# Rectified row sums: clamping on ScalarE and summing on VectorE, four rows per instruction, with three input buffers

## The chip, the cores and the metric

The kernel runs on one core of one Trainium2 chip. The metric is the device time of one execution in microseconds.

## The reference

```python
def setup_inputs():
    batch, seq, dim = 32, 512, 1024
    return {"x": np.random.randn(batch, seq, dim).astype(np.float32)}

def reference(x):
    relu_x = np.maximum(x, 0)
    return np.sum(relu_x, axis=-1).astype(np.float32)
```

There are 16,384 rows of 1024 fp32 numbers, 67.1 MB. Each of the 128 partitions takes 128 rows that follow one another in memory.

## The kernel before

Seven blocks of 16 rows per partition (4 KB a row, so 64 KB per partition) go through two buffers. Then come pieces of 8, 4, 2 and 1 rows, and the last row in four parts. Even rows go to ScalarE, odd rows to VectorE; each row is one instruction that clamps and sums. The sums gather in `res`, one column per row.

```python
io_pool = ctx.enter_context(tc.tile_pool(name="io", bufs=2))
# ... act_op: scalar.activation(Relu, accum_out=res[:, m])
# ... dve_op: vector.tensor_scalar(max 0, add, accum_out=...)
for j, cpd in enumerate(chunks):                 # 16 x 7, then 8, 4, 2, 1
    # ... xt = a buffer of the pool
    nc.sync.dma_start(out=xt, in_=...)
    for c in range(cpd):
        m = m0 + c
        if m == NT - 2:                          # row 126, ScalarE's last
            act_op(xt[:, c, :], xt[:, c, :], m)
            nc.scalar.dma_start(out=out2d[:, 0 : NT - 2], in_=res[:, 0 : NT - 2])
        elif (c % 2) == 0:
            act_op(xt[:, c, :], xt[:, c, :], m)
        else:
            dve_op(xt[:, c, :], xt[:, c, :], res[:, m : m + 1])
    m0 += cpd
# ... row 127 in four parts on VectorE
nc.sync.dma_start(out=out2d[:, NT - 2 : NT], in_=res[:, NT - 2 : NT])
```

The scheduler puts ScalarE's output DMA ahead of ScalarE's last row. In ScalarE's stream stand, one after the other, a separate semaphore wait (an instruction of its own that does nothing but wait for another engine's signal; the trace has it at 158.38 us, 0.02 us long) for VectorE's last full row (row 13 of the tail, row 125 in all), the issue of the output DMA, and row 126.

## Time and profile before

| | before |
|---|---|
| device time | 164.37 us (164.32 to 164.52) |
| span | 162.7 us |
| load queue busy | 96.4% of 16 DMA engines' span |
| VectorE, ScalarE busy | 46%, 42% |
| last load packet ends | 159.3 us |
| last output DMA issued | 160.44 us |

From the page of the kernel before: span and busy times, the DMA queues (packets, MB, share), the chain that ended last by engine, and the two main groups of instructions (count, busy us, mean ns of one, idle before and what ended it).

```profile
span 162.7 us, 347 instructions
DVE 74.3 (46%) x134; ACT 69.0 (42%) x129; POOL 0.2 (0%) x4
...
q1 hardware_dynamic: 2304, 67.11, 96.4%
q10 hardware_dynamic: 144, 0.06, 0.1%
q14 instruction: 2, 0.02, 0.0%
...
DMA 78%; DVE 18%; SPq 1%; issue 0%; DVEq 0%
...
L49 DVE TENSOR_SCALAR_CACHE_REDUCE xt<-xt 128x1024 f32<-128x1024 f32 x63 | 72.6, 1215 | 85.7 <-DMA xt<-in_x_dram 85.4
L41 ACT ACTIVATE xt<-xt 128x1024 f32<-128x1024 f32 x64 | 66.7, 1043 | 90.3 <-DMA xt<-in_x_dram 90.3
```

The loads (q1) fill the span, and both engines wait for them more than they work.

The end of the timeline of the kernel before (start us, duration us, engine, line, operation; ACTq and SPq are DMA issues):

```profile
158.44 0.37 ACTq L73 DMA_DIRECT2D out_dram<-res  x1
...
158.85 1.06 ACT L41 ACTIVATE xt<-xt 128x1024 f32<-128x1024 f32 x1 [0.58 <-DMA xt<-in_x_dram]
...
159.82 0.19 ACT L41 ACTIVATION_READ_ACCUMULATOR xt<-xt 128x1 f32 x1
...
160.29 0.08 DVE L49 DVE_READ_ACCUMULATOR p<-p 128x1 f32 x1
160.44 0.35 SPq L98 DMA_DIRECT2D out_dram<-res  x1
```

ScalarE ends its last row at 160.0, VectorE its last part at 160.37, and the last output goes out at once.

### The profile page before, as it was taken

The numbers are of one execution on the slowest core, as the hardware profiler recorded it, in microseconds if no ns is written. First come the engines' busy times: TensorE is split into PE (matmuls) and PEld (weight loads), VectorE is DVE, ScalarE is ACT, GpSimd is POOL, SyncE is SP. The second block draws the span as 40 slices with busy tenths as digits, with TensorE's granted clock in tenths as the row PEclk, the third lists the DMA queues.
The fourth block names the chain that finished last, engine by engine and source line by source line (L and its number), as shares of the span: only waits on it lengthen the run. The fifth ranks groups of instructions, "written<-read, shape, count | busy, mean of one in ns | idle before, by whom it ended". The sixth has DMA issues, their size and how long they took to land.

```text
span 162.7 us, 347 instructions
## 1 busy us (share of the span) xinstructions
DVE 74.3 (46%) x134; ACT 69.0 (42%) x129; POOL 0.2 (0%) x4
## 2 busy tenths in 40 slices
DVE  0000029900597007950099300992039900598983
ACT  3000029700595007930099100990039700596882
POOL 0000000000000000000000000000000000000000
DMA  7969969969969979979989998998997997999990
GB/s 258 483 290 516 499 274 516 499 274 516 500 274 516 516 306 467 516 338 435 516 356 421 499 403 387 516 419 354 516 467 306 516 467 306 451 443 395 405 362 23
DMA packets 2450, 67.19 MB, mean 413 GB/s; under 512 B 528, under 2 KB 1040, under 8 KB 1168
## 3 DMA queue, kind: packets, MB, share of 16 engines
q1 hardware_dynamic: 2304, 67.11, 96.4%
q10 hardware_dynamic: 144, 0.06, 0.1%
q14 instruction: 2, 0.02, 0.0%
HBM read 67.11 MB, written 0.07 MB: 413 GB/s over the span
## 4 chain that ended last, share of the span: by engine, by line
DMA 78%; DVE 18%; SPq 1%; issue 0%; DVEq 0%
DMA xt<-in_x_dram 62%; DVE xt L49 17%; DMA p<-in_x_dram 17%; SPq L65 1%; DVE p L49 1%; DVEq L49 0%; DVEq L124 0%
## 5 line engine op out<-in xcount | busy, mean ns | idle before, releaser
L49 DVE TENSOR_SCALAR_CACHE_REDUCE xt<-xt 128x1024 f32<-128x1024 f32 x63 | 72.6, 1215 | 85.7 <-DMA xt<-in_x_dram 85.4
L41 ACT ACTIVATE xt<-xt 128x1024 f32<-128x1024 f32 x64 | 66.7, 1043 | 90.3 <-DMA xt<-in_x_dram 90.3
L41 ACT ACTIVATION_READ_ACCUMULATOR xt<-xt 128x1 f32 x64 | 11.9, 186 | 0.0
L49 DVE DVE_READ_ACCUMULATOR xt<-xt 128x1 f32 x63 | 5.2, 83 | 0.0
L49 DVE TENSOR_SCALAR_CACHE_REDUCE p<-p 128x244 f32<-128x244 f32 (+3 forms) x4 | 1.6, 420 | 0.5 <-DMA p<-in_x_dram 0.4
L41 ACT ACT_TABLE_LOAD x1 | 1.3, 1283 | 0.7 <-PEq L113 0.7
L49 DVE DVE_READ_ACCUMULATOR p<-p 128x1 f32 x4 | 0.3, 83 | 0.0
L113 POOL MEMSET const-bfloat16-1.0<- 128x1 bf16 x1 | 0.1, 102 | 0.0
L113 POOL MEMSET const-uint8-127<- 128x1 uint8 x1 | 0.1, 101 | 0.0
L113 POOL MEMSET const-float32-0.0<- 128x1 f32 x1 | 0.1, 99 | 0.2 <-issue 0.2
L113 POOL MEMSET const-float32-1.0<- 128x1 f32 x1 | 0.1, 98 | 0.0
## 6 DMA issues: line engine op xcount, KB each, us to landing
xt<-in_x_dram SPq DMA_DIRECT2D x1, 4096.0 KB, 19.7
xt<-in_x_dram SPq DMA_DIRECT2D x1, 2048.0 KB, 24.2
xt<-in_x_dram SPq DMA_DIRECT2D x1, 1024.0 KB, 26.2
xt<-in_x_dram SPq DMA_DIRECT2D x1, 512.0 KB, 27.0
p<-in_x_dram SPq DMA_DIRECT2D x1, 134.0 KB, 10.0
p<-in_x_dram SPq DMA_DIRECT2D x1, 130.0 KB, 26.5
p<-in_x_dram SPq DMA_DIRECT2D x1, 126.0 KB, 26.7
p<-in_x_dram SPq DMA_DIRECT2D x1, 122.0 KB, 26.9
```

The lines of the kernel that those rows point to most:

```text
L41: nc.scalar.activation(out=out_ap, in_=in_ap, func=mybir.ActivationFunctionType.Relu, accum_out=res[:, m : m + 1],)
L49: nc.vector.tensor_scalar(out=out_ap, in0=in_ap, scalar1=0.0, scalar2=None, op0=mybir.AluOpType.max, op1=mybir.AluOpType.add, accum_out=ac ...
L65: nc.sync.dma_start(out=xt, in_=xv[:, m0 * D : (m0 + cpd) * D].rearrange("p (c d) -> p c d", c=cpd),)
L113: nc = _bacc.Bacc("TRN2", target_bir_lowering=False, num_devices=1)
```

## The change

The intent is fewer and longer instructions, with the buffer room to let the two engines work one behind the other. In six of the eight blocks ScalarE clamps four rows in one instruction (128x4096), and VectorE sums these four rows in one `tensor_reduce`. Since a buffer is then held longer, there are three of 64 KB in place of two. Block 6 and the tail keep the row instructions; the tail's pieces share one of the three buffers. The core of the diff (helpers renamed and the last row's parts are cut):

```diff
-    io_pool = ctx.enter_context(tc.tile_pool(name="io", bufs=2))
+    io = ctx.enter_context(tc.tile_pool(name="io", bufs=3))
...
+    for j in range(nbig):
+        m0 = j * ROWS
+        xt = io.tile([P, ROWS, D], fp32, tag="io", name=f"xt{j}")
+        nc.sync.dma_start(out=xt, in_=xv[:, m0 : m0 + ROWS, :])
+        if j < nbig - 1:
+            for c in range(0, ROWS, STEP):
+                rows = xt[:, c : c + STEP, :]
+                nc.scalar.activation(
+                    out=rows, in_=rows, func=mybir.ActivationFunctionType.Relu
+                )
+                nc.vector.tensor_reduce(
+                    out=res[:, m0 + c : m0 + c + STEP],
+                    in_=rows,
+                    axis=mybir.AxisListType.X,
+                    op=mybir.AluOpType.add,
+                )
         else:
+            # block 6: rows by turns, as before
...
+        if c0 + n == ROWS - 1:
+            nc.scalar.dma_start(out=out2d[:, : NT - 2], in_=res[:, : NT - 2])
```

## The prediction

> **What bounds the kernel now.** The input stream. The DMA queue table shows the load queue busy for 96.4% of the 162.7 us span (67.11 MB, 413 GB/s); only the start and the last 3.5 us lack DMA. The chain of waits is 78% DMA. Its 17% on VectorE only says that a buffer release issued a load; that load still had about 10 us of an earlier one in front of it (a 4 MB load takes 29.5 us from issue to landing, but one lands every 19.5 us: 23.2, 42.7, ... 120.75, 140.1). Both engines are half idle: per 16-row block each works about 9.2 us (timeline: VectorE rows 1.14 us apart, ScalarE rows 1.04 us apart), then waits 10 us for DMA.
>
> **What the change does in blocks 0 to 5.** It removes 48 row instructions and their accumulator reads on each engine, and adds 24 ScalarE clamps (128x4096) and 24 VectorE sums (128x4096), one behind the other; each engine now touches every row.
> - A clamp: the trace has 1.040 us for 1024 elements.[...]
> - A sum: the trace's pitch for 1024 elements is 1.14 us[...].[...] Estimate: 4.35 us each, 17.4 us a block, starting 3.6 us after the landing: buffer free 21 us after landing, against 9.2 now.
>
> VectorE's 17.4 us still fits the 19.5 us block period. A release 21 us after landing would starve two buffers, but there are three: load j+3 is issued about 21 us after block j landed, when block j+2 still has some 18 us to run. So the stream stays unbroken: same bytes, same pieces, no gain in DMA time, the only thing to gain.
>
> **The tail.** Block 5 lands at 120.75; VectorE ends its sums near 141.9 (124.4 + 4 x 4.35), 1.7 us after block 6 landed. From there VectorE is continuously busy: block 6 rows to 151, the 8-row piece to 155.6, 4-row to 157.9, row 13 to 159.0 (before: 158.35). The large output DMA on ScalarE's queue waits for row 13, and ScalarE's last row stands behind it: it ends near 160.6 (before 160.0); the four pieces on VectorE near 160.5 (before 160.37). The last output is issued 0.2 to 0.4 us later. Every 0.1 us more per sum adds 0.4 us here.
>
> **Prediction:** 164.8 us, range 164.2 to 166.0. Faster by over 2%: 1%; within 2%: 94%; slower by over 2%: 5%.
>
> **What would show it.** Right: load queue still busy about 96%, a 4 MB landing every 19.5 us; loads landing about 40 us after issue; clamps near 3.6 us, sums near 4.35 us; VectorE busy about 127 us, ScalarE about 107 us; VectorE's first row of block 6 about 1.7 us late.
> Wrong: sums over 4.87 us (19.5 / 4): VectorE then falls behind at each block, takes over the chain, and the time rises over 2%. Or clamps waiting for sums of the same tile (8 us per four rows, 32 us a block); the built order shows no such wait. Or DMA packets that slow down while both engines sweep each tile. Or faster landings from three queued loads, which I do not expect: the DMA engines already have no pauses.

The forecast's clamp, the "3.6 us after the landing", was 3.60 us, 3.51 us apart, 14.1 us a block, not shown then. The 4.35 us of a sum is close to what the row instructions of VectorE in the trace of the kernel before give as an estimate, 4.32 us for 4096 elements (the next one starts 1.14 us after a row of 1024 elements and 0.33 us after a part of 244, so 1.04 ns an element and 0.08 us for each). That `tensor_reduce` keeps this pace was an assumption, not shown then. With 3.6 us and four times 4.35 us, VectorE ends block 5's sums near 141.9 us, the last output comes 0.2 to 0.4 us later, and the forecast came to 164.8 us, 0.4 above the 164.4 of the kernel before.

## More of the kernel before

The issue of the large output DMA takes 0.37 us of ScalarE's queue.

## The result and the profile after

The changed kernel is correct and takes 166.16 us (166.14 to 166.17), against 164.34 us for the kernel before in the same rounds. Ratios here are the mean time of one kernel's fast runs over that of the other's of the same rounds, so not quite the ratio of the medians that are quoted: 1.0113, 95% interval 1.0099 to 1.0127. That is inside 2%, but above the predicted range of 164.2 to 166.0, and the rise of 1.8 us is about four times the predicted 0.4.

The page after:

```profile
span 164.4 us, 203 instructions
DVE 123.0 (75%) x62; ACT 103.3 (63%) x57; POOL 0.2 (0%) x4
...
q1 hardware_dynamic: 2304, 67.11, 95.3%
q10 hardware_dynamic: 144, 0.06, 0.1%
q14 instruction: 2, 0.02, 0.0%
...
L70 DVE TENSOR_REDUCE res<-xt 128x4 f32<-128x4096 f32 x24 | 104.4, 4412 | 36.6 <-ACT xt L67 36.6
L67 ACT ACTIVATE xt<-xt 128x4096 f32<-128x4096 f32 x24 | 84.8, 3604 | 47.3 <-DMA xt<-in_x_dram 47.3
```

Up to the tail all is as predicted: a clamp takes 3.60 us and a sum 4.41 us, VectorE still waits before each of the blocks 0 to 5 (36.6 us in six waits), and the loads are about as dense as before (load queue busy 95.3% of the span in place of 96.4%; a block lands every 19.4 us in place of 19.5). By the DMA records the last load packet even ends at 158.9 us, 0.4 us earlier than in the profile of before. The time is lost behind that point. The end of the chain of waits after (start us, us, what; ACTq is ScalarE's queue, "issue" is time without a wait that the profile shows):

```profile
150.13 7.99 DVE tail L48 x14
158.13 0.02 issue
158.15 0.02 ACTq L96
158.16 0.35 issue
158.51 2.37 ACTq L96
160.88 0.05 issue
160.93 1.06 ACT tail L40
161.98 0.09 ACTq L138
```

And the end of the timeline after:

```profile
158.51 2.37 ACTq L96 DMA_DIRECT2D out_dram<-res  x1
...
159.90 0.08 DVE L48 DVE_READ_ACCUMULATOR p<-p 128x1 f32 x1
160.93 1.06 ACT L40 ACTIVATE tail<-tail 128x1024 f32<-128x1024 f32 x1 [3.05 <-DVE p L48]
161.89 0.19 ACT L40 ACTIVATION_READ_ACCUMULATOR tail<-tail 128x1 f32 x1
162.10 0.35 SPq L112 DMA_DIRECT2D out_dram<-res  x1
```

VectorE is done at 159.98, earlier than before (160.37). ScalarE's issue of the output DMA, the same 63 KB as before, takes 2.37 us in place of 0.37, and a gap of 0.35 us precedes it. ScalarE's last row stands behind that issue, and the last output behind the row: it is issued at 162.10 in place of 160.44. The note "3.05 <-DVE p L48" on the last row misleads: ScalarE did not need VectorE's parts, it was in its own queue's DMA issue.

What went on during the issue? The DMA queues of the changed kernel between 158.5 and 160.9 us:

```profile
q14 instruction: 1, 0.01, 1.4%
q1 hardware_dynamic: 14, 0.01, 1.3%
```

One packet of q14 falls into the issue; its record gives 8,192 bytes, from 159.17 to 159.72 us. In the kernel before, both q14 packets came near 85 and 88 us. The trace calls their kind "instruction". So I took them for refills of the engines' instruction streams. "Refill" below is my name for such a packet: no trace shows what it carries, but the experiments test the reading by moving the packets.

Counted in the trace from 0, the held issue is instruction 63 of ScalarE (an accumulating activation counts as two, as in the trace). Before, it was number 136. So the theory was: the change made ScalarE's stream shorter, and by that moved a refill from the middle of the kernel onto the issue at its end. The rival: something else in the changed kernel (third buffer, deeper load queue, sums written in strips) makes the issue long.

### The profile page after: what moved, and what is told of

It is laid out like the page before. It is cut to its first block, busy times and chain, and to the rows that moved or that the text cites. A ratio compares the mean times of both kernels' runs of the same rounds, so it can differ in the third digit from the quotient of the medians.

```text
span 164.4 us, 203 instructions
## 1 busy us (share of the span) xinstructions
DVE 123.0 (75%) x62; ACT 103.3 (63%) x57; POOL 0.2 (0%) x4
## 3 DMA queue, kind: packets, MB, share of 16 engines
q1 hardware_dynamic: 2304, 67.11, 95.3%
## 4 chain that ended last, share of the span: by engine, by line
DMA 48%; DVE 30%; ACT 14%; another core or an unknown queue 3%; issue 2%; ACTq 2%; SPq 0%
DMA xt<-in_x_dram 48%; DVE res L70 20%; ACT xt L67 13%; DVE xt L48 5%; DVE tail L48 5%; ACTq L96 1%; ACT tail L40 1%; SPq L62 0%; ACTq L138 0%; ACTq L67 0%
## 5 line engine op out<-in xcount | busy, mean ns | idle before, releaser
L70 DVE TENSOR_REDUCE res<-xt 128x4 f32<-128x4096 f32 x24 | 104.4, 4412 | 36.6 <-ACT xt L67 36.6
L67 ACT ACTIVATE xt<-xt 128x4096 f32<-128x4096 f32 x24 | 84.8, 3604 | 47.3 <-DMA xt<-in_x_dram 47.3
L40 ACT ACTIVATE tail<-tail 128x1024 f32<-128x1024 f32 x8 | 8.4, 1048 | 5.6 <-DVE p L48 3.0
L40 ACT ACTIVATE xt<-xt 128x1024 f32<-128x1024 f32 x8 | 8.3, 1042 | 5.2 <-DMA xt<-in_x_dram 5.2
L48 DVE TENSOR_SCALAR_CACHE_REDUCE xt<-xt 128x1024 f32<-128x1024 f32 x8 | 9.2, 1212 | 0.0
L48 DVE TENSOR_SCALAR_CACHE_REDUCE tail<-tail 128x1024 f32<-128x1024 f32 x7 | 8.1, 1213 | 0.0
L48 DVE TENSOR_SCALAR_CACHE_REDUCE p<-p 128x244 f32<-128x244 f32 (+3 forms) x4 | 1.5, 420 | 0.3 <-DMA p<-in_x_dram 0.3
L40 ACT ACTIVATION_READ_ACCUMULATOR tail<-tail 128x1 f32 x8 | 1.5, 186 | 0.0
L40 ACT ACTIVATION_READ_ACCUMULATOR xt<-xt 128x1 f32 x8 | 1.5, 186 | 0.0
L48 DVE DVE_READ_ACCUMULATOR xt<-xt 128x1 f32 x8 | 0.7, 82 | 0.0
L48 DVE DVE_READ_ACCUMULATOR tail<-tail 128x1 f32 x7 | 0.6, 81 | 0.0
L48 DVE DVE_READ_ACCUMULATOR p<-p 128x1 f32 x4 | 0.3, 83 | 0.0
```

What stands on the lines that cost most here:

```text
L40: nc.scalar.activation(out=ap, in_=ap, func=mybir.ActivationFunctionType.Relu, accum_out=res[:, m : m + 1],)
L48: nc.vector.tensor_scalar(out=ap, in0=ap, scalar1=0.0, scalar2=None, op0=mybir.AluOpType.max, op1=mybir.AluOpType.add, accum_out=accum_out,)
L67: nc.scalar.activation(out=rows, in_=rows, func=mybir.ActivationFunctionType.Relu)
L70: nc.vector.tensor_reduce(out=res[:, m0 + c : m0 + c + STEP], in_=rows, axis=mybir.AxisListType.X, op=mybir.AluOpType.add,)
```

## The experiments

"Place" is the number of a traced ScalarE instruction, from 0. The q14 records don't name an engine; a refill is put down to ScalarE where it moves with ScalarE's places while VectorE's stream is unchanged. The edits are shortened here.

### Move the issue: e1, e2, e3 (edits of the changed kernel)

```diff
# e1_pad8: eight tiny activations at the start of ScalarE's stream
+    nc.gpsimd.memset(pad_in, 0.0)
+    for i in range(8):
+        nc.scalar.activation(out=pad_out[:, i : i + 1], in_=pad_in, func=Relu)
# e2_few4: in blocks 0 to 3, one clamp of eight rows for the first two of four
-   two activations on xt[:, 0:4, :] and xt[:, 4:8, :]
+   one activation on xt[:, 0:8, :]
# e3_out_sp: the output DMA leaves ScalarE's stream
-            nc.scalar.dma_start(out=out2d[:, : NT - 2], in_=res[:, : NT - 2])
+    nc.sync.dma_start(out=out2d[:, : NT - 2], in_=res[:, : NT - 2])  # behind the last load
```

> The changed kernel with eight one-element activations added at the start of ScalarE's stream, where ScalarE waits 21 us for the first block anyway. Refill theory (a refill of ScalarE's instruction stream falls on the output DMA's issue, because that issue is the 64th traced instruction of ScalarE): with eight more in front the refill falls eight instructions before it, among the tail rows; the output DMA's issue goes back from 2.37 us to about 0.37, and the time to 164.0 to 164.4. State theory (something else of the changed kernel, such as the deeper load queue or the sums written in strips of four, makes that issue long): it stays 2.4 us, and the time 166.2.

> The changed kernel with four ScalarE instructions fewer: in blocks 0 to 3 one clamp of eight rows in place of two of four; VectorE's sums are unchanged. Refill theory: the output DMA's issue is now about the 60th instruction, so the refill comes behind ScalarE's last row; the issue takes 0.37 us, time 164.0 to 164.5[...]. State theory: the issue stays 2.4 us, the time 166.2.

> The changed kernel with the large output DMA issued from SyncE's queue, behind the last load, so that ScalarE's stream has no DMA issue. Refill theory: no issue is held; ScalarE's last row starts when its data is there, and the time is 164.0 to 164.5; if a refill holds any instruction and not a DMA issue alone, the last row or its accumulator read is up to 2 us late and the time near 166. State theory: SyncE's issue of the same transfer is long too, the final output waits behind it, and the time is 166 or more.

| run | place of the issue | issue, us | time, us | ratio to before (95%) |
|---|---|---|---|---|
| changed kernel | 63 | 2.37 | 166.16 | 1.0113 (1.0099 to 1.0127) |
| e1_pad8 | 71 | 0.37 | 164.22 | 1.0007 (0.9990 to 1.0025) |
| e2_few4 | 59 | 0.37 | 164.59 | 1.0026 (1.0009 to 1.0044) |
| e3_out_sp | none (SyncE: 0.35) | - | 164.30 | 1.0006 (0.9983 to 1.0028) |

The timeline of e1_pad8 at the end:

```profile
158.29 0.37 ACTq L106 DMA_DIRECT2D out_dram<-res  x1
158.71 1.06 ACT L50 ACTIVATE tail<-tail 128x1024 f32<-128x1024 f32 x1 [0.89 <-DVE tail L58]
```

Clamps, sums, buffers and loads are as in the changed kernel, and the 1.8 us are gone; in e1 with eight instructions *more*. The rival falls. In e1 both q14 packets come near 153 us; in e2 the second comes at 160.67 us, behind ScalarE's last row.

### Bring it about in the kernel before: e4 and e10

```diff
# e4_before_pad55 (e10_before_pad56: 56 in place of 55), on the kernel before
+    nc.gpsimd.memset(pad_in, 0.0)
+    for i in range(55):
+        nc.scalar.activation(out=pad_out[:, i : i + 1], in_=pad_in, func=Relu)
```

> The kernel before with 55 one-element activations at the start of ScalarE's stream, which moves its output DMA's issue from place 136 to 191 (counted from 0), that is 63 + 128[...]. Refill theory: a refill shows near 158 to 159 us, the issue takes 2.4 us, and the time rises from 164.3 to about 166.0. State theory, or padding without effect: issue 0.37 us, time 164.3.

> The kernel before with 56 in place of 55 added activations, the neighbour of the run that reproduced the long issue. The separate wait, not the issue, now stands in place 191. Place theory and wait theory both: issue 0.37 us, time 164.0 to 164.6, so that one activation of 0.19 us more saves 1.7 us. If the added activations themselves cost the time: near 166.0 as with 55. Wait theory also: the second refill of ScalarE no longer shows near 158.8 us but some us earlier, while its sequencer stands at the wait.

e4 took 166.00 us, ratio 1.0120 (1.0097 to 1.0143), e10 164.39 us, ratio 1.0014 (0.9999 to 1.0029). The end of e4:

```profile
158.11 2.24 ACTq L83 DMA_DIRECT2D out_dram<-res  x1
160.40 1.06 ACT L51 ACTIVATE xt<-xt 128x1024 f32<-128x1024 f32 x1 [2.75 <-DVE p L59]
```

and of e10, with one instruction more:

```profile
158.37 0.37 ACTq L83 DMA_DIRECT2D out_dram<-res  x1
158.79 1.06 ACT L51 ACTIVATE xt<-xt 128x1024 f32<-128x1024 f32 x1 [0.58 <-DMA xt<-in_x_dram]
```

So the loss arises in a kernel that has nothing of the change (1.9 us by the medians of e4's rounds, 166.00 against 164.09), and one more tiny activation takes it away. The critical places are 63 and 191, 128 apart. The step of 128 was my assumption when e4 was planned, with no trace to show it; the 2.24 us of the issue in place 191 bear it out. As expected of e10, ScalarE's second refill came at 153.35 in place of 158.78 us.

### Its neighbours: e5 and e6

```diff
# e5_few1: in block 0 alone, one clamp of eight rows for the first two of four
-   two activations on xt[:, 0:4, :] and xt[:, 4:8, :]
+   one activation on xt[:, 0:8, :]
# e6_pad1: one tiny activation at the start
+    nc.gpsimd.memset(pad_in, 0.0)
+    nc.scalar.activation(out=pad_out, in_=pad_in, func=Relu)
```

> The changed kernel with one ScalarE instruction fewer (one clamp of eight rows in block 0), so that not the output DMA's issue but the instruction behind it, ScalarE's last row, stands where the issue stood in the changed kernel (place 63 of the traced instructions, counted from 0). Theory A (the refill holds whatever instruction stands there): the issue takes 0.37 us, the last row starts about 2 us late, time near 166. Theory B (a DMA issue alone is held, other instructions are not): issue 0.37 us, the last row starts right behind it, time 164.0 to 164.6.

> The changed kernel with one one-element activation more at the start of ScalarE, so that the wait ahead of the output DMA's issue stands in that place and the issue one behind it. Theory A: the wait or the issue behind it is held, the last row is again 1.5 to 2 us late, time 165.7 to 166.2. Theory B: issue 0.37 us, time 164.0 to 164.6.

e5 took 164.13 us, ratio 0.9992 (0.9977 to 1.0007), e6 164.14 us, ratio 0.9995 (0.9980 to 1.0009); both issues took 0.37 us. Theory B holds here. In e5 the refill (159.50) came behind the issue, and ScalarE's last row in place 63 started 0.38 us after the issue's end, in place of 0.05 in e6. So the row instruction that stands in that place in e5 lost only this gap, 0.33 us. In e6 there was no refill at the end at all: both q14 packets came near 153.2 us. That was not explained yet: if the refill is due at place 63, and the separate wait stood there until 158.2, why 153.2?

### Amid the stream of loads: e7 and e8, a miss

```diff
# e7_mid_ctl: an early DMA behind ScalarE's clamps of block 1
+            if j == 1:
+                nc.scalar.dma_start(out=probe, in_=xt[:, ROWS - 1, : NT - 2])
# e8_mid_hit: the same, with 52 tiny activations at the start
```

> The changed kernel with one small DMA more (126 columns of a clamped row to a scratch tile), issued by ScalarE behind its clamps of block 1, when it has some 5 us to wait; this is the control for the next run. This early issue should take 0.37 us. It also moves the output DMA one place on, as in the run with one activation more: Theory A a time near 166, Theory B 164.0 to 164.6.

> The same with 52 one-element activations at the start of ScalarE, so that the early DMA's issue, near 57 us and amid the load stream, stands in that place (63), and the output DMA at the end far from it. Refill theory: the early issue is held, by 2 us or, if the refill queues behind the loads' 2.4 us packets, up to 5 us; it falls into ScalarE's wait for block 2, so the time stays 164.0 to 164.6; the output DMA's issue takes 0.37 us. If the long issue belongs to the end of the kernel and not to the place: the early issue takes 0.37 us.

The early issue took 0.52 us in e7 (0.37 expected) and 0.51 in e8, where it stands in place 63. So the place alone does not do it. The refill of e8 came at 9.79 us, while ScalarE still waited for its first block, in place 55. The times, 165.80 and 165.95 us (ratios 1.0090 and 1.0106), were a second miss: I expected no change. Their load stream itself was late: block 4 landed complete at 102.3 and 102.1 us, against 100.1 in the changed kernel. The chain of waits of e7 (start us, us, what) shows what it waited for:

```profile
56.57 22.35 DMA probe<-xt
...
78.99 23.65 DMA xt<-in_x_dram
```

Amid the loads the early DMA took 22.35 us to land. It reads the buffer of block 1, and block 4 is loaded into that buffer. So this load was issued at 78.99 us (79.35 in e8) in place of 63.55, when only block 3 was still on its way, and that landed at 80.98. This is read from the traces; no run took the dependence away. The times say nothing of the hold on an issue.

e6 and e8 suggested a sharper theory: ScalarE's sequencer runs ahead over instructions for the engine, even ones that will wait, and starts the refill when it comes to the place, and a separate semaphore wait stops it. It is inferred from the times of the refills alone (near 153.2 us in e6, 9.79 us in e8); no trace shows how far the sequencer is. In the changed kernel such a wait, for VectorE's row 13, stands right in front of place 63, so by this theory the refill could not start before 158.16 us; its packet came at 159.17.

### The separate wait: e9 and e11

```diff
# e9_carry: the wait on row 13 is carried by a tiny activation
+            nc.scalar.activation(out=carry, in_=res[:, NT - 3 : NT - 2], func=Relu)
             nc.scalar.dma_start(out=out2d[:, : NT - 2], in_=res[:, : NT - 2])
# e11_carry2: as e9, and this activation waits for GpSimd too
+    nc.gpsimd.memset(carry, 0.0)
```

> The changed kernel in which the separate semaphore wait on VectorE's row 13, ahead of the output DMA's issue, is replaced by a one-element activation that reads that row's sum and so carries the wait; the issue keeps its place (63). Place theory (an issue in that place is held, whatever is ahead of it): issue about 2.4 us, time near 166. Wait theory (the refill starts when ScalarE's sequencer comes to that place; instructions for the engine itself, waiting or not, are passed on ahead of time, but a separate semaphore wait stops it, and in the changed kernel it stopped right in front of the place until row 13 was done): the refill comes early, near 153 us, and is done by then; issue 0.37 us, time 164.0 to 164.6.

> As the carry run, but the carrying activation also waits for GpSimd, so that the separate wait on row 13 comes back ahead of it: wait in place 62, activation in 63, output DMA's issue in 64. The refill then starts right behind the wait, about 0.2 to 0.6 us before the issue. If an issue is held by any refill in flight: 1.7 to 2.4 us, time 165.7 to 166.4. If only an issue that itself stands in the place is held: 0.37 us, time 164.2 to 164.9.

In e9 the issue stands in place 63 as in the changed kernel, and nothing else differs but the kind of wait in place 62:

```profile
158.41 0.20 ACT L97 ACTIVATE carry<-res 128x1 f32<-128x1 f32 x1
158.41 0.37 ACTq L102 DMA_DIRECT2D out_dram<-res  x1
158.83 1.06 ACT L41 ACTIVATE tail<-tail 128x1024 f32<-128x1024 f32 x1 [0.22 <-ACT carry L97]
```

The issue takes 0.37 us, the time is 164.37 us, ratio 1.0011 (0.9992 to 1.0030), and the q14 packets come at 153.15 and 153.77 us. In e11 the separate wait is back, the tiny activation has place 63 and the issue place 64:

```profile
158.63 0.20 ACT L98 ACTIVATE carry<-res 128x1 f32<-128x1 f32 x1 [0.52 <-DVE tail L50]
158.66 2.12 ACTq L103 DMA_DIRECT2D out_dram<-res  x1
```

The issue is held 2.12 us though it is not itself in the place; the time is 166.40 us, ratio 1.0139 (1.0119 to 1.0158). Its refill packet came at 159.28 to 159.69 us, during the issue. So in these runs it is a refill under way that holds the issue, and the separate wait that makes the refill late (159.28 us in e11, 153.77 at the latest in e9).

### Which issue is held: e12 to e15

```diff
# e12_mid_wait: the early DMA to SBUF in place 63 (51 tiny activations), behind a
#   separate wait on a VectorE copy:
+                if j == 1 and c == 2 * STEP:
+                    nc.vector.tensor_copy(out=probe, in_=xt[:, 0, : NT - 2])
+            if j == 1:
+                nc.scalar.dma_start(out=probe, in_=xt[:, ROWS - 1, : NT - 2])
# e13_mid_dram: the same arrangement, but it writes to DRAM (overwritten at the end)
+                nc.scalar.dma_start(out=out2d[:, 16:32], in_=...)   # 16 columns of xt
# e14_end_sbuf, changed kernel: a copy to SBUF in front of the output DMA
+            nc.scalar.dma_start(out=probe, in_=res[:, : NT - 2])
             nc.scalar.dma_start(out=out2d[:, : NT - 2], in_=res[:, : NT - 2])
# e15_one_output, changed kernel: two clamps fewer, one output DMA at the very end
-    nc.sync.dma_start(out=out2d[:, NT - 2 : NT], in_=res[:, NT - 2 : NT])
+    nc.scalar.dma_start(out=out2d, in_=res)
```

> The early DMA amid the load stream again, in place 63, but now with a separate semaphore wait in place 62, on a VectorE copy that ends near 59.3 us, after ScalarE's clamps of block 1 (56.6). Wait theory: the refill, which came at 9.8 us without that wait, now comes about 1 us after 59.3, and the issue is held 2 us or more (up to 5 if the refill queues behind the loads' 2.4 us packets). If the hold belongs to the end of the kernel: the issue takes 0.4 to 0.5 us. The time is no test here: this early DMA cost the load stream 1.6 us in its two former runs.

> The early DMA in place 63 behind a separate wait, as in the run before, but it writes 16 columns to the output in DRAM (values that the last output DMA overwrites) in place of SBUF. If the destination decides: the issue, near 60 us, is held 2 us or more. If the place in the stream of loads decides: 0.4 to 0.5 us, the refill again several us later.

> The changed kernel with a copy of the sums to an SBUF tile issued ahead of the output DMA, so that this SBUF write and not the DRAM write stands in place 63 behind the separate wait, near 158.3 us; ScalarE's last row follows in 64 and the output DMA in 66. If the destination decides: the copy's issue takes 0.5 us, time 164.5 to 165.5. If the end of the kernel decides: the copy's issue is held, 2.1 to 2.5 us, and the last row with it, time 166 to 167.

> The changed kernel with one output DMA for everything, issued by ScalarE behind VectorE's last piece near 160.3 us, when the load stream (159.0) is over; two ScalarE instructions fewer put this issue again in place 63 behind a separate wait. If a hold needs loads in flight: issue 0.37 us, time about 164.5. If not: the refill starts about 1.0 us behind the wait and the issue is held 2.0 to 2.4 us, time about 166.5.

e12 was half a miss. The refill did come late (65.78 us, behind the wait's end at 59.81), but the issue was not held:

```profile
60.17 0.50 ACTq L89 DMA_DIRECT2D probe<-xt  x1
```

e13 writes to DRAM in the same arrangement (8 KB in place of 63, and the wait ends later, at 63.72), and ScalarE stands for 5.6 us:

```profile
63.50 0.16 DVE L86 COPY xt<-xt 128x8 f32<-128x8 f32 x1
64.07 5.62 ACTq L91 DMA_DIRECT2D out_dram<-xt  x1
69.73 3.62 ACT L76 ACTIVATE xt<-xt 128x4096 f32<-128x4096 f32 x1 [13.06 <-issue]
```

e14 has both kinds one after the other at the end. The SBUF write in place 63 passes, and the DRAM write two places on is held:

```profile
158.51 0.50 ACTq L97 DMA_DIRECT2D probe<-res  x1
...
159.07 1.06 ACT L41 ACTIVATE tail<-tail 128x1024 f32<-128x1024 f32 x1 [1.10 <-DVE p L49]
159.11 1.75 ACTq L98 DMA_DIRECT2D out_dram<-res  x1
```

(The parts of the row are what the profile names as releaser again; the copy's issue and the 0.35 us gap stood ahead.) The closest comparison is this copy with the held issue of the changed kernel: the same place, source, bytes and start (158.51 us), but 0.50 us to SBUF and 2.37 us to DRAM. Here ScalarE's last row is in front of the held issue, and the hold costs less: 164.94 us, ratio 1.0046 (1.0004 to 1.0088). In e15 the load stream is over (158.9), and the issue is held all the same:

```profile
160.33 2.25 ACTq L116 DMA_DIRECT2D out_dram<-res  x1
```

It took 166.41 us, ratio 1.0135 (1.0106 to 1.0165). The times of e12 and e13 (167.60 and 167.69 us, ratios 1.0206 and 1.0213, neither clearly over 2%) are no test of the hold, as was said of e12 in advance. Their loss is twice that of e7, by the same dependence: the load of block 4 was issued at 82.01 and 81.56 us, when block 3 had already landed (81.36 and 80.91) and no load was on its way.

The refill packets (from the DMA records) and the six held issues, in us:

| run | separate wait ends | refill packet | held issue ends | after the packet's end |
|---|---|---|---|---|
| changed kernel | 158.16 | 159.17 to 159.72 | 160.88 | 1.16 |
| e4_before_pad55 | 157.78 | 158.78 to 159.26 | 160.35 | 1.09 |
| e11_carry2 | 158.27 | 159.28 to 159.69 | 160.78 | 1.09 |
| e13_mid_dram | 63.72 | 68.15 to 68.46 | 69.69 | 1.23 |
| e14_end_sbuf | 158.16 | 159.16 to 159.69 | 160.85 | 1.16 |
| e15_one_output | 159.99 | 160.98 to 161.45 | 162.58 | 1.13 |

At the end of the kernel the packet starts 1.0 us behind the wait; amid the loads, whose packets of 64 KB take 2.42 us each (median in the trace of the changed kernel), 4.4 us (e13) or 6.0 us (e12). All six held issues write to DRAM, and they end 1.1 to 1.2 us after the packet's end.

## Why the prediction was right or wrong

- **The bound and the gain: right.** The kernel is bound by its loads (load queue busy 96.4% of the span before, 95.3% after), and the change takes nothing from them. Without the hold it runs within 0.3% of the kernel before (e1, e2, e5, e6, e9).
- **The costs of the new instructions: right.** Clamps 3.60 us (3.60 predicted), sums 17.40 us a block (17.4). A sum keeps the pace of the row instructions, as assumed: 16,384 elements in 17.40 us are 0.94 per ns, against 0.90 for a row (1024 in 1.14 us). VectorE frees block 0 at 44.2 us, 21 us after its landing, as predicted; a load of a block lands 37.0 us after its issue (about 40 predicted). The prediction's "4 MB" for such a load is a slip, since 16 rows are 8.4 MB; nothing rests on it. The sums of busy time, "about 127" and "about 107", were 4 us too high (123.0 and 103.3): I added instructions that overlap.
- **Serialised clamps, slower packets, faster landings: right to leave out.** No clamp waited for a sum: the clamps of a block are 3.51 us apart, and their 47.3 us of idle time all ended with a load. The packets of 64 KB took 2.42 us (median) before and after, and a block landed every 19.5 and 19.4 us.
- **VectorE's backlog in the tail: right in length, harmless in effect.** VectorE starts block 6 1.6 us late (1.7 predicted), and from block 5's landing to the end of row 13 it takes 38.1 us (38.25 predicted: 159.0 - 120.75). But block 5 landed at 119.98 in this profile, not at 120.75, and the last row's parts landed only after VectorE had caught up.
- **The step that failed** reads: "The large output DMA on ScalarE's queue waits for row 13, and ScalarE's last row stands behind it: it ends near 160.6". The order is right, and so is the dependence of the last output. What was mis-sized is the issue between them: I carried over its 0.37 us from the kernel before. It measured 2.37 us, with a gap of 0.35 us ahead, and ScalarE's last row ended at 162.08, though row 13 was done earlier (158.11) than the 159.0 predicted. The last output was issued 1.66 us later than before, in place of the predicted 0.2 to 0.4. Had the issue not held ScalarE, VectorE's end at 159.98 would have decided, an estimate of about 2.0 us earlier than 162.10; the loads' earlier end in this profile hid 0.4 us of the loss.
- **The cause, by runs:** ScalarE's stream lost 73 places before the issue, so a refill fell just there (e1, e2, e4, e5, e10); behind the separate wait on VectorE it came late (159.17 us in the changed kernel and 159.28 in e11, against 153.77 at the latest in e9); and the issues that write to DRAM were held by such a refill, while those that write to SBUF were not (5.62 us in e13 against 0.50 in e12; 2.37 in the changed kernel against 0.50 in e14). I had not looked at the instruction packets.
- **Open:** why the DRAM writes were held and the SBUF writes were not (the SBUF writes tried were copies from SBUF; a load from DRAM was not tried); what sets the first place to 63, of which these programs show just one value; and why the small DMA amid the loads took 22 us to land (22.35 in e7, 22.60 in e8). No run pointed to a version faster than both kernels: with the hold gone and nothing added amid the loads, the changed kernel took 164.13 to 164.59 us (e1, e2, e3, e5, e6, e9), ratios 0.9992 to 1.0026.

## What to carry to other kernels

Where a change adds or removes instructions on an engine that also issues DMAs, look at the instruction packets in the DMA queues before and after: here a refill that cost nothing visible in the middle (85 and 88 us; ScalarE's rows stayed 1.04 us apart) came to fall on an issue at the end (159.17 us) and cost 1.8 us. If a DRAM-writing issue suddenly takes 2 us (2.37 here in place of 0.37), move it by a few places (e1, e2: 0.37 us), give it to another queue (e3: 0.35), or let an engine instruction carry the wait ahead of it (e9: 0.37); each of the three took the loss away here, the last only where no separate wait was left (e9, but not e11: 2.12). Look too at what a small added DMA reads: in e7 the next load into the buffer that it read was issued only when it had landed, 22.35 us after its issue, and the time rose to 165.80 us. And before you explain a small loss by the change itself, bring the loss about in the unchanged kernel.

## What the runs measured of refills and small DMAs

- The q14 packets inside the spans have 8,192 bytes, and the two places in which an output issue was held are 128 apart (63 in the changed kernel, 191 in e4). Right behind a separate wait in front of the place the gap was 0.33 to 0.36 us (changed kernel, e4, e12 to e15; 0.04 in the kernel before), and a DRAM-writing issue behind it took 1.75 to 2.37 us at the end of a kernel (5.62 us amid loads, e13) in place of 0.37.
- The runs fit a refill that starts early past engine instructions that will still wait, but not past a separate semaphore wait: its packet had started by 153.8 us in e9 and came at 159.17 us in the changed kernel.
- The issue on ScalarE's queue, where it was not held, took 0.34 to 0.38 us to DRAM and 0.50 to 0.52 us for copies from SBUF to SBUF; in these runs only issues to DRAM were held.
- A small DMA from ScalarE amid the load stream took 22.35 us to land (63 KB, e7), against 1.6 us for the 63 KB that the kernel before writes at its end.
